# A transformer layer's token sums, load queues, memory norm and weight copies rearranged

## The chip, the cores and the metric

The kernel is one program on one core of a Trainium2 chip. The metric is device microseconds (us) from the start to the end of an execution; lower is better. A core has five engines, each with its own instruction stream: TensorE (PE in the profile; PEld is its weight loads), VectorE (DVE), ScalarE (ACT), GpSimd (POOL) and SyncE (SP). SP computes nothing here: it issues DMAs, which 16 DMA engines carry out. POOL and ACT can issue DMAs as well. An instruction waits on semaphores until its inputs are there, and everything behind it on its engine waits with it.

## The reference, cut to what matters

One layer on a sequence of 1024 tokens and width 1024, in float32: token mixing (a diagonal state-space branch and an eight-head attention with forget gates, each normalised, then one output projection), cross-attention into 256 memory tokens, and a gated feed-forward part.

```python
def rms_norm(x, g):
    return x * lax.rsqrt(jnp.mean(x * x, axis=-1, keepdims=True) + RMS_EPS) * g

mem_n = rms_norm(mem, mem_g)                       # 256 x 1024
proj = rms_norm(x, mix_pre_g) @ w_in               # u | q | k | v | f
y_ssm = s5_mixer(u, ...)                           # ends in a GLU, 512 channels
y_fox = forgetting_attention(q, k, v, f_logit)     # 8 heads x 64 = 512 channels
y_mix = concatenate([rms_norm(y_ssm, ssm_out_g), rms_norm(y_fox, fox_out_g)])
x = x + rms_norm(y_mix @ w_out, mix_post_g)
x = x + rms_norm(memory_cross_attention(rms_norm(x, xa_pre_g), mem_n, wq, wkv, wo), xa_post_g)
x = x + rms_norm(swiglu(rms_norm(x, ffn_pre_g), w_gate, w_up, w_down), ffn_post_g)
```

The two `rms_norm` of the branches need, for each token, the sum of squares over 512 channels. In this kernel the channels lie on partitions, so that sum runs over partitions, and PE makes it: a matmul of 128 tokens' squares with a column of ones.

## The kernel before, in words

Float32 products are made of three matmuls: `split` writes a high part (ACT, L113) and a low part (DVE, L115, or L117 with a gain), and `mm3` (L122 to L124) multiplies high by high, high by low and low by high. So a weight tile goes DMA, ACT, DVE, PE. Tiles have 128 partitions and mostly 512 columns.

A scheduler puts the instructions of each engine in an order from the program's order, priorities and its own costs; `tc.issue_after(x)` keeps what is issued under it behind instruction `x`. The stages, by the times of the profile:

- **0 to 50 us, start-up.** `u_part` multiplies each of eight row blocks of `xT` with a 128x512 block of `w_u`, loaded on SP (`u_load`, L262; `x_fetch`, L205) as PE goes along.
- **50 to 285 us, projections.** `in_proj` makes q, k and v (`qk_tile`, `v_tiles`; q and k go to `qk_d` in DRAM) beside the state-space work. `mem_stats` squares the memory tokens and makes their scale `r_mem`.
- **200 to 500 us, attention.** `fox` goes through 64 units (8 heads `h` x 8 blocks `t` of 128 queries). For a unit, `scores` has PE multiply q and k (L742, L743), DVE add the bias and take the extreme (L749), ACT make the exponentials (L751), and DVE or POOL divide by their sum (L756, L754); then `turn` transposes the unit on PE (L769) and `values` multiplies by v (L780) for each pair of units. `prepare(h + 1)` loads the next head's q and k halves into a buffer with the tag "e", and the bias row `ncb`, on SP (L712, L720, L721). Between units run **fillers**, in this order: the rest of v, `glu` (the GLU of the state-space branch), `mem_load` (loads `memT`, multiplies it by the tokens' scales, L958, and splits it), 16 tiles of `mem_tile` (memory times `wkv`, each result stored to `kv_d` on SP, L972), and rows of `out_ssm` (the state-space half of the output projection, stored to `t1_d` on SP, L854).
- **500 to 593 us, output projection.** For each token block PE multiplies into an x buffer in PSUM; DVE takes it out with the scale `r_f` (L1044), ACT squares it (L1045). Blocks of `build_a(1)` and products with `wo` run between.
- **593 to 785 us, cross-attention** over eight token blocks `j`; `xa_prep(j)` loads the block from `x1_d` (L1069, SP).
- **785 to 1438 us, feed-forward.** `hid` and `wd_sums` prepare combined blocks: `wd_sums` also copies 33 blocks of `w_down` of 256 KB from DRAM to DRAM, to `wd_d` (L1339, SP). These copies depend on nothing, and the scheduler issues them in the start-up.

Squares before: in `glu`, each of eight steps (4 channel blocks `ct` x 2 halves `h`) squares its 128 channels, and `token_sums` makes four matmuls per step (L237), whose result DVE adds to `sv_s` (L239, L241). In `fox`, heads 0 and 1 do the same with two matmuls for each `values`; heads 2 and 3 write squares, and heads 4 to 7 add theirs on POOL (L801) into one tile "d", whose eight sums are taken at the end, before `r_f` can be made.

Of the kernel before, what the change touches and what calls it, by code (L numbers as in the profile page):

```python
# [52 lines left out]
def layer(ctx: ExitStack, tc: tile.TileContext, a, out):  # L53
# [95 lines left out]
    stA, stB, stC = pool, sp, pool  # L149
# [33 lines left out]
    t1_d = dram.tile([L, NC, D], F32, name="t1_d")  # L183
    kv_d = dram.tile([16, P, 256], F32, name="kv_d")
# [48 lines left out]
    def token_sums(sv, sq, first, p0=0, p1=P):  # L233
        n = sv.shape[1]
        ps = g_ps([P, n])
        for j in range(n):
            pe.matmul(ps[:, j:j + 1], sq[:, j * P:(j + 1) * P], ones[p0:p1, 0:1], start=True, stop=True)  # L237
        if first:
            dve.tensor_copy(sv, ps)  # L239
        else:  # L240
            dve.tensor_tensor(out=sv, in0=ps, in1=sv, op=ALU.add)  # L241
# [421 lines left out]
    def glu(ys):  # L663
# [7 lines left out]
        sv = const.tile([P, NT], F32, name="sv_s")  # L671
        sq, sums = tt("d"), []
        for ct in range(4):
            cs = slice(ct * P, (ct + 1) * P)
            hl = slab([P, 2, S])
            for h in range(2):
                hs = slice(h * 512, h * 512 + 512)
# [9 lines left out]
                while sums:  # L687
                    token_sums(*sums.pop())
                act.activation(out=sq[:, hs], in_=y, func=AF.Square)
                sums.append((sv[:, 4 * h:4 * h + 4], sq[:, hs], ct == 0))  # L690
                if h == 1:
                    ys.append(hl)
                yield
        token_sums(*sums.pop())
        ys_stat.append(sv)

    def glu_stats():
        sv, = ys_stat
        tables("natural_log_exp_and_others")
        rsqrt_mean(r_s, sv, 512, 4 * EPS)  # L700


    def fox(yf):
# [3 lines left out]
        def prepare(h):  # L707
# [4 lines left out]
            sp.dma_start(out=ncb, in_=nc_d[h:h + 1, :].broadcast_to([P, S]))  # L712
            heads[h] = (qs, ka, ncb)
            eng = dve if h < 2 else pool
            for hf in range(2):
                hs = slice(hf * 512, hf * 512 + 512)
                qk = tt("d" if h == 0 and hf else "e", [P, 2, 512])
                qd, kd = qk[:, 0], qk[:, 1]
                for rr in (0, 64):
                    sp.dma_start(out=qd[rr:rr + 64], in_=qk_d[h // 2, r0:r0 + 64, hs])  # L720
                    sp.dma_start(out=kd[rr:rr + 64], in_=qk_d[4 + h // 2, r0:r0 + 64, hs])  # L721
                yield
                with behind():
                    act.activation(out=qs[:, hs], in_=qd, func=AF.Copy)
                    eng.tensor_tensor(out=qs[64:128, hs], in0=qd[64:128], in1=qs[64:128, hs].bitcast(F32),
                                      op=ALU.subtract)
                    split(ka[:, 0, hs], ka[:, 1, hs], kd, lo_eng=eng)

        last = []
# [4 lines left out]
        def scores(h, t):  # L734
# [18 lines left out]
            if t in POOL_T and h > 1:  # L753
                pool.tensor_tensor(out=sc[:, :ke], in0=sc[:, :ke], in1=rl.broadcast_to([P, ke]), op=ALU.mult)  # L754
# [17 lines left out]
        def values(h, qc):  # L772
# [17 lines left out]
            if h < HA:  # L790
                act.activation(out=sq, in_=y, func=AF.Square)
                later.append((sv[:, 2 * qc:2 * qc + 2], sq, h == 0, 64 - r0, P - r0))
                return
            if h == HA and qc == 0:
                sums.append(tt("d"))
            total = sums[0][64 - r0:P - r0, qs_]
            if h < HA + 2:
                act.activation(out=total, in_=y, func=AF.Square)
            else:
                act.activation(out=sq, in_=y, func=AF.Square)  # L800
# [35 lines left out]
        while later:  # L836
            token_sums(*later.pop(0))
# [760 lines left out]
```

## Time and profile before

| | |
|---|---|
| Time, median of 3 runs | 1434.43 us (1434.07 to 1434.55) |
| The profiled execution, whole | 1440.18 us |
| Its span (first to last instruction) | 1438.4 us |
| PE busy | 1395.6 us, 97% |
| DVE busy | 1002.3 us, 70% |
| ACT busy | 705.6 us, 49% |
| POOL busy | 398.4 us, 28% |
| Data moved by DMA | 238.42 MB, mean 166 GB/s |

A row such as `60.4 1.36 PE L122 MATMUL g<-whl,slab` has a start, a duration, the engine, the line, the operation and the tiles written and read; a bracket behind it has the idle time just before it and what ended that idle time. A matmul's duration reaches beyond the next one's start, since they are pipelined: what one costs is the distance between starts. `SPq` is a DMA issue on SP. PEclk is the clock that PE was granted, 1.00 being full.

### The profile page before, as it was taken

Reading aid. Unit: us, or ns where it says so; the run is one execution under the profiler, and the core shown is the slowest. Engines: PE = TensorE matmul, PEld = TensorE weight load, DVE = VectorE, ACT = ScalarE, POOL = GpSimd, SP = SyncE. Lnnn points to the kernel's source line nnn. Section 1 sums busy time; section 2 is a strip of 40 time slices with the busy share of each in tenths; the row PEclk is TensorE's granted clock in tenths of the full one; section 3 lists DMA queues with packets and bytes.
Section 4 is the critical chain, followed back from the end, with each engine's and each line's share of the span. In section 5 each row is a group of like instructions: output and inputs, shape, how many; then the busy total and the mean of one; then the engine's idle time right before and its main releaser. Section 6 shows DMA issues by size and latency. Waiting matters only on the chain.

```text
span 1438.4 us, 20783 instructions
## 1 busy us (share of the span) xinstructions
PE 1395.6 (97%) x7422; PEld 1191.4 (83%) x7422; DVE 1002.3 (70%) x1818; ACT 705.6 (49%) x1389; POOL 398.4 (28%) x432
## 2 busy tenths in 40 slices
PE   7999999999999899999999999999999899999997
PEld 6789898889989886788888788888888788888886
DVE  7848957887788877645457677777775766565565
ACT  6363347777888754543434533333333234444441
POOL 0000000022243135001021367667656621000021
PEclk9999999999999999999999999999999999999999
DMA  9625763165644658202327355554455425966544
GB/s 312 216 73 145 201 191 124 39 196 183 194 147 118 172 156 285 91 30 72 105 88 247 134 183 183 183 182 151 166 191 183 146 95 202 339 213 197 176 161 161
DMA packets 112823, 238.42 MB, mean 166 GB/s; under 512 B 11848, under 2 KB 48712, under 8 KB 112592
## 3 DMA queue, kind: packets, MB, share of 16 engines
q1 hardware_dynamic: 96576, 182.01, 39.2%
q0 software_dynamic: 16144, 55.09, 10.8%
q8 instruction: 58, 0.95, 0.3%
q14 instruction: 45, 0.37, 0.1%
HBM read 168.90 MB, written 76.81 MB: 171 GB/s over the span
## 4 chain that ended last, share of the span: by engine, by line
PE 59%; DMA 13%; DVE 11%; POOL 6%; issue 5%; ACT 5%; SPq 1%; DVEq 0%; POOLq 0%; ACTq 0%
PE x L1271 7%; PE x L1526 7%; PE g L1526 7%; PE g L1271 6%; PE g L122 6%; PE g L124 5%; PE g L123 5%; DMA wt<-in_w_down 5%; DMA wt_d<-wt 4%; POOL wt L1345 3%; PE x L123 2%; PE x L124 2%; PE x L122 2%; PE g L769 1%; ACT slab L113 1%
## 5 line engine op out<-in xcount | busy, mean ns | idle before, releaser
L1271 PE MATMUL x<-slab,op 128*128 128x512 f32 x984 | 235.2, 391 | 4.2 <-ACT ev L1287 3.6
L1271 PEld LDWEIGHTS x<-slab,op 128*128 128x128 f32 x984 | 185.7, 189 | 43.8 <-ACT ev L1287 4.1
L1271 PE MATMUL g<-slab,op 128*128 128x512 f32 x744 | 178.7, 389 | 0.0
L115 DVE TENSOR_TENSOR slab<-slab 128x1024 fp32r<-128x1024 f32 (+2 forms) x92 | 110.4, 1208 | 82.3 <-ACT slab L113 80.8
L1271 PEld LDWEIGHTS g<-slab,op 128*128 128x128 f32 x744 | 139.7, 188 | 29.0
L122 PE MATMUL g<-slab,whl 128*128 128x512 f32 (+1 forms) x416 | 151.6, 364 | 0.8 <-DVE slab L115 0.4
L123 PE MATMUL g<-slab,whl 128*128 128x512 f32 (+1 forms) x416 | 148.4, 357 | 0.0
L124 PE MATMUL g<-slab,whl 128*128 128x512 f32 (+1 forms) x416 | 148.0, 357 | 0.0
L113 ACT ACTIVATE slab<-slab 128x1024 fp32r<-128x1024 f32 (+2 forms) x92 | 95.0, 1037 | 104.4 <-DMA slab<-hs_d 81.2
L1526 PE MATMUL g<-slab 128*128 128x512 f32 x462 | 126.6, 389 | 0.0
L1526 PE MATMUL x<-slab 128*128 128x512 f32 x462 | 126.6, 389 | 0.0
L1526 PEld LDWEIGHTS g<-slab 128*128 128x128 f32 x462 | 86.7, 188 | 18.0
L1526 PEld LDWEIGHTS x<-slab 128*128 128x128 f32 x462 | 86.7, 188 | 18.0
L122 PE MATMUL g<-whl,slab 128*128 128x256 f32 (+2 forms) x288 | 86.0, 311 | 11.9 <-ACT whl L113 9.5
L1345 POOL TENSOR_TENSOR wt<-wt 128x256 f32<-128x256 f32 x88 | 73.3, 833 | 73.0 <-DMA wt<-in_w_down 70.6
L113 ACT ACTIVATE op<-ss 128x512 fp32r<-128x512 f32 x60 | 37.6, 629 | 106.3 <-PE g L1271 45.4
L115 DVE TENSOR_TENSOR whl<-raw,whl 128x1024 fp32r<-128x1024 f32 (+2 forms) x61 | 71.9, 1182 | 24.1 <-ACT whl L113 23.7
L122 PEld LDWEIGHTS g<-slab,whl 128*128 128x128 f32 x416 | 78.6, 189 | 12.1 <-ACT whl L113 0.6
L124 PEld LDWEIGHTS g<-slab,whl 128*128 128x128 f32 x416 | 78.4, 189 | 11.6 <-DVE whl L115 0.2
L123 PEld LDWEIGHTS g<-slab,whl 128*128 128x128 f32 x416 | 78.7, 189 | 10.5
L113 ACT ACTIVATE op<-slab 128x512 fp32r<-128x512 f32 x80 | 49.8, 626 | 76.6 <-PE x L1271 40.0
L123 PE MATMUL g<-whl,slab 128*128 128x256 f32 (+2 forms) x288 | 86.7, 301 | 0.0
(394 smaller groups left out, 3192.2 us busy)
## 6 DMA issues: line engine op xcount, KB each, us to landing
hs_d<-ev POOLq DMA_DIRECT2D x77, 256.0 KB, 3.0
slab<-hs_d SPq DMA_DIRECT2D x35, 512.0 KB
wt<-in_w_down SPq DMA_DIRECT2D x44, 256.0 KB
wt_d<-wt POOLq DMA_DIRECT2D x22, 512.0 KB, 3.5
slab<-in_w_gate SPq DMA_DIRECT2D x20, 512.0 KB
slab<-in_w_up SPq DMA_DIRECT2D x20, 512.0 KB
slab<-wt_d SPq DMA_DIRECT2D x20, 512.0 KB
wd_d<-in_w_down SPq DMA_DIRECT2D x33, 256.0 KB
```

Source lines behind the costliest of these rows:

```text
L113: first = act.activation(out=hi, in_=src, func=AF.Copy, scale=1.0 if mul is None else mul)
L115: (lo_eng or dve).tensor_tensor(out=lo, in0=src, in1=hi.bitcast(F32), op=ALU.subtract)
L122: pe.matmul(ps, lh, rh, start=first, stop=False)
L123: pe.matmul(ps, lh, rl, start=False, stop=False)
L124: pe.matmul(ps, ll, rh, start=False, stop=last)
L769: pe.transpose(tp[:, k], sc[:, (k0 + k) * P:(k0 + k + 1) * P], ident)
L1271: pe.matmul(ps, x[:, k], y[:, k], start=first and k + n == 0, stop=k == 3 and n == 2, skip_group_check=not first)
L1345: pool.tensor_tensor(out=o, in0=x, in1=y, op=ALU.subtract)
L1526: pe.matmul(banks[n][j], xo[:, u, js], wo[:, v], start=ends[0] and k == 0, stop=ends[1] and k == 2, skip_group_check=onto is not None)
```

## The change

The program's text changes in these places:

1. **Squares are summed over partitions once.** `glu` goes through its steps half by half; the squares of the four channel blocks are added on DVE in the tile `sq`, and `glu_sums(h)` takes four sums per half. `glu_stats(h)` makes `r_s` half by half, between rows of `out_ssm`. In `fox`, heads 0 and 1 store their squares to `sq_d`, head 2 reads them back as the tile "d", and every later head adds its own on POOL; the sums are taken in the last head, and `r_f` is made in two parts, columns 0 to 5 and 6 to 7.
2. **Queues.** `stB` is ACT, so the 16 stores to `t1_d` (some of the stores of `out_ssm`) and 16 to `kv_d` are issued by ACT. For heads 1 to 7 the loads of q, k and the bias are issued by POOL, as four loads of 64x1024 and the row; from head 3 on they stand behind POOL's multiplication of unit `t` = 1 (`mults`). k lands in the low half of `ka` and is split in place.
3. **Memory norm ahead.** `mem_norm` scales `memT` within `in_proj`, by the tokens' scales on DVE and the gains on ACT, and stores it to `mem_d` on POOL; `mem_load` only loads and splits it.
4. **Copies.** The 33 copies of `w_down` are issued on SP behind the loads of `x1` for blocks 0 to 5.

```diff
-    stA, stB, stC = pool, sp, pool
+    stA, stB, stC = pool, act, pool
...
-    def token_sums(sv, sq, first, p0=0, p1=P):
+    def token_sums(sv, sq):
         n = sv.shape[1]
         ps = g_ps([P, n])
         for j in range(n):
-            pe.matmul(ps[:, j:j + 1], sq[:, j * P:(j + 1) * P], ones[p0:p1, 0:1], start=True, stop=True)
-        if first:
-            dve.tensor_copy(sv, ps)
-        else:
-            dve.tensor_tensor(out=sv, in0=ps, in1=sv, op=ALU.add)
+            pe.matmul(ps[:, j:j + 1], sq[:, j * P:(j + 1) * P], ones[:, 0:1], start=True, stop=True)
+        dve.tensor_copy(sv, ps)
...
-        sv = const.tile([P, NT], F32, name="sv_s")
-        sq, sums = tt("d"), []
-        for ct in range(4):
-            cs = slice(ct * P, (ct + 1) * P)
-            hl = slab([P, 2, S])
-            for h in range(2):
-                hs = slice(h * 512, h * 512 + 512)
+        sq = tt("d")
+        ys_stat.extend((const.tile([P, NT], F32, name="sv_s"), sq))
+        for h in range(2):
+            hs = slice(h * 512, h * 512 + 512)
+            for ct in range(4):
+                cs = slice(ct * P, (ct + 1) * P)
+                if h == 0:
+                    ys.append(slab([P, 2, S]))
+                hl = ys[ct]
...
-                while sums:
-                    token_sums(*sums.pop())
-                act.activation(out=sq[:, hs], in_=y, func=AF.Square)
-                sums.append((sv[:, 4 * h:4 * h + 4], sq[:, hs], ct == 0))
-                if h == 1:
-                    ys.append(hl)
+                act.activation(out=y if ct else sq[:, hs], in_=y, func=AF.Square)
+                if ct:
+                    dve.tensor_tensor(out=sq[:, hs], in0=sq[:, hs], in1=y, op=ALU.add)
+                if (h, ct) == (1, 1):
+                    glu_sums(0)
                 yield
-        token_sums(*sums.pop())
-        ys_stat.append(sv)
-
-    def glu_stats():
-        sv, = ys_stat
-        tables("natural_log_exp_and_others")
-        rsqrt_mean(r_s, sv, 512, 4 * EPS)
+
+    def glu_sums(h):
+        sv, sq = ys_stat
+        token_sums(sv[:, 4 * h:4 * h + 4], sq[:, 512 * h:512 * h + 512])
+
+    def glu_stats(h):
+        hs = slice(4 * h, 4 * h + 4)
+        rsqrt_mean(r_s[:, hs], ys_stat[0][:, hs], 512, 4 * EPS)
...
-            sp.dma_start(out=ncb, in_=nc_d[h:h + 1, :].broadcast_to([P, S]))
...
+            qd, kd = tt("e"), ka[:, 1].bitcast(F32) if h else tt("d")
+            with tc.issue_after(mults[-1].ins) if mults else ExitStack():
+                for rr in (0, 64):
+                    for t_, i in ((qd, 0), (kd, 4)):
+                        (pool if h else sp).dma_start(out=t_[rr:rr + 64], in_=qk_d[i + h // 2, r0:r0 + 64])
+                (pool if h else sp).dma_start(out=ncb, in_=nc_d[h:h + 1, :].broadcast_to([P, S]))
             for hf in range(2):
                 hs = slice(hf * 512, hf * 512 + 512)
-                qk = tt("d" if h == 0 and hf else "e", [P, 2, 512])
-                qd, kd = qk[:, 0], qk[:, 1]
-                for rr in (0, 64):
-                    sp.dma_start(out=qd[rr:rr + 64], in_=qk_d[h // 2, r0:r0 + 64, hs])
-                    sp.dma_start(out=kd[rr:rr + 64], in_=qk_d[4 + h // 2, r0:r0 + 64, hs])
                 yield
                 with behind():
-                    act.activation(out=qs[:, hs], in_=qd, func=AF.Copy)
-                    eng.tensor_tensor(out=qs[64:128, hs], in0=qd[64:128], in1=qs[64:128, hs].bitcast(F32),
+                    act.activation(out=qs[:, hs], in_=qd[:, hs], func=AF.Copy)
+                    eng.tensor_tensor(out=qs[64:128, hs], in0=qd[64:128, hs], in1=qs[64:128, hs].bitcast(F32),
                                       op=ALU.subtract)
-                    split(ka[:, 0, hs], ka[:, 1, hs], kd, lo_eng=eng)
-
-        last = []
+                    split(ka[:, 0, hs], ka[:, 1, hs], kd[:, hs], lo_eng=eng)
+
+        last, mults = [], []
...
-                pool.tensor_tensor(out=sc[:, :ke], in0=sc[:, :ke], in1=rl.broadcast_to([P, ke]), op=ALU.mult)
+                mults.append(pool.tensor_tensor(out=sc[:, :ke], in0=sc[:, :ke], in1=rl.broadcast_to([P, ke]), op=ALU.mult))
...
-            if h < HA:
-                act.activation(out=sq, in_=y, func=AF.Square)
-                later.append((sv[:, 2 * qc:2 * qc + 2], sq, h == 0, 64 - r0, P - r0))
+            act.activation(out=sq, in_=y, func=AF.Square)
+            if h < 2:
+                stC.dma_start(out=sq_d[64 - r0:P - r0, qs_], in_=sq)
                 return
-            if h == HA and qc == 0:
+            if h == 2 and qc == 0:
                 sums.append(tt("d"))
+                stC.dma_start(out=sums[0], in_=sq_d)
             total = sums[0][64 - r0:P - r0, qs_]
-            if h < HA + 2:
-                act.activation(out=total, in_=y, func=AF.Square)
-            else:
-                act.activation(out=sq, in_=y, func=AF.Square)
-                pool.tensor_tensor(out=total, in0=total, in1=sq, op=ALU.add)
+            pool.tensor_tensor(out=total, in0=total, in1=sq, op=ALU.add)
+            if h == NH - 1:
+                later.append((sv[:, 2 * qc:2 * qc + 2], sums[0][:, qs_]))
...
-                    if len(later) > 1 or h >= HA and later:
+                    if len(later) > 1:
                         token_sums(*later.pop(0))
-        while later:
-            token_sums(*later.pop(0))
-        token_sums(sv, sums[0], False)
-        rsqrt_mean(r_f, sv, 512)
+        rsqrt_mean(r_f[:, 0:6], sv[:, 0:6], 512)
+        token_sums(*later.pop(0))
+        rsqrt_mean(r_f[:, 6:8], sv[:, 6:8], 512)
...
+    def mem_norm(r):
+
+        rb = row_bcast(r, 2)
+        for k in range(0, KT, 2):
+            m = t2t([P, 2, 256])
+            sp.dma_start(out=m, in_=a["memT"].rearrange("(k p) m -> p k m", p=P)[:, k:k + 2])
+            dve.tensor_tensor(out=m, in0=m, in1=bc(rb, 1, 2), op=ALU.mult)
+            for i in range(2):
+                act.activation(out=m[:, i], in_=m[:, i], func=AF.Copy, scale=g_mem[:, k + i:k + i + 1])
+            stA.dma_start(out=mem_d[:, k:k + 2], in_=m)
+
...
+            if i == 2:
+                mem_norm(r)
...
-    def mem_load(r, out):
-        rb = row_bcast(r, 2)
-        yield
+    def mem_load(out):
         mh, ml = slab([P, KT, 256]), slab([P, KT, 256])
         for k in range(0, KT, 4):
             m = raw([P, 4, 256])
-            sp.dma_start(out=m, in_=a["memT"].rearrange("(k p) m -> p k m", p=P)[:, k:k + 4])
-            dve.tensor_tensor(out=m, in0=m, in1=bc(rb, 1, 4), op=ALU.mult)
-            for kk in range(4):
-                split(mh[:, k + kk], ml[:, k + kk], m[:, kk], g_mem[:, k + kk:k + kk + 1])
-                if kk % 2:
-                    yield
+            sp.dma_start(out=m, in_=mem_d[:, k:k + 4])
+            split(mh[:, k:k + 4], ml[:, k:k + 4], m)
+            yield
...
-        glu_stats()
-        for _ in mem_load(r_mem[0], mem):
+        tables("natural_log_exp_and_others")
+        glu_stats(0)
+        for h in range(2):
+            for _ in range(2):
+                step(rows)
+                yield
+            if h == 0:
+                glu_sums(1)
+                glu_stats(1)
+        for _ in mem_load(mem):
...
-        sp.dma_start(out=x1, in_=x1_d[j])
+        x1_read.append(sp.dma_start(out=x1, in_=x1_d[j]))
...
-            sp.dma_start(out=wd_d[f, h, p], in_=a["w_down"][2 * p + f][:, h * 512:h * 512 + 512])
+            with tc.issue_after(x1_read[min(k // 4, 5)].ins):
+                sp.dma_start(out=wd_d[f, h, p], in_=a["w_down"][2 * p + f][:, h * 512:h * 512 + 512])
```

What this does to the order of instructions is shown at three places, without the rows' numbers.

SP in the start-up, from the copies on (`wd_d`), `in_w_u` being the blocks for `u_part`, `in_xT` the row blocks of `xT`, `h_d` a small store; before:

```order
L1339 DMA wd_d<-in_w_down 128x512 x6
L205 DMA slab<-in_xT 128x1024
L262 DMA raw<-in_w_u 128x512
L205 DMA slab<-in_xT 128x1024
L1339 DMA wd_d<-in_w_down 128x512 x3
L262 DMA raw<-in_w_u 128x512
L1339 DMA wd_d<-in_w_down 128x512 x14
L262 DMA raw<-in_w_u 128x512
L1339 DMA wd_d<-in_w_down 128x512 x4
L262 DMA raw<-in_w_u 128x512
L1339 DMA wd_d<-in_w_down 128x512 x6
```

And of the change, from the same `h_d` store on (lines are those of the changed text):

```order
L551 DMA h_d<-c 128x112
L207 DMA slab<-in_xT 128x1024
L261 DMA raw<-in_w_u 128x512
L207 DMA slab<-in_xT 128x1024
L261 DMA raw<-in_w_u 128x512 x3
L158 DMA raw<-in_w_f 128x1024
L876 DMA raw<-in_mem 128x1024 x2
```

The 33 copies are gone from between the loads; the last three blocks of `w_u` follow each other, and the weights and memory tokens of the next stage follow them.

SP at the turn to cross-attention, where `x_d` is `x1_d`, `in_post_g` a gain row and `in_wo` the weights of the cross-attention's output; before:

```order
L1069 DMA c<-x_d 128x1024
L948 DMA d<-in_post_g 128x1024
L1069 DMA c<-x_d 128x1024
L158 DMA raw<-in_wo 128x1024 x2
L1069 DMA c<-x_d 128x1024 x5
```

And of the change:

```order
L1084 DMA c<-x_d 128x1024
L1355 DMA wd_d<-in_w_down 128x512
L960 DMA d<-in_post_g 128x1024
L1355 DMA wd_d<-in_w_down 128x512 x2
L158 DMA raw<-in_wo 128x1024
L1084 DMA c<-x_d 128x1024
L1355 DMA wd_d<-in_w_down 128x512 x5
L158 DMA raw<-in_wo 128x1024
L1355 DMA wd_d<-in_w_down 128x512 x4
L1084 DMA c<-x_d 128x1024
```

Three copies now stand ahead of the last but one load of `in_wo`, eight ahead of the last; the rest follow the later blocks' loads.

DVE at the end of attention, from a split of `whl` (weights) on; `sv_f` are the sums, `rst` and `rsv` steps of `r_f`, L1044 takes a block of the output projection out of PSUM; before:

```order
L115 TENSOR_TENSOR whl<-raw,whl 128x1024
L788 TENSOR_TENSOR yt<-g,yt 64x256
L115 TENSOR_TENSOR whl<-raw,whl 128x1024
L117 SCALAR_TENSOR_TENSOR slab<-yt,gains,slab 64x256
L115 TENSOR_TENSOR whl<-raw,whl 128x1024
L241 TENSOR_TENSOR sv_f<-g,sv_f 128x8
L139 TENSOR_SCALAR rsv<-sv_f 128x8
L143 TENSOR_TENSOR rst<-rsy 128x8
L144 TENSOR_TENSOR rst<-rst,rsv 128x8
L117 SCALAR_TENSOR_TENSOR slab<-g,gains,slab 128x256
L145 SCALAR_TENSOR_TENSOR r_f<-rst,rsy 128x8
L1044 SCALAR_TENSOR_TENSOR a<-x,r_f,a 128x512 x2
```

And of the change, where L240 takes the sums out and L1059 is the former L1044:

```order
L240 COPY sv_f<-g 128x2
L139 TENSOR_SCALAR rsv<-sv_f 128x6
L115 TENSOR_TENSOR whl<-raw,whl 128x1024
L143 TENSOR_TENSOR rst<-rsy 128x6
L144 TENSOR_TENSOR rst<-rst,rsv 128x6
L145 SCALAR_TENSOR_TENSOR r_f<-rst,rsy 128x6
L1059 SCALAR_TENSOR_TENSOR a<-x,r_f,a 128x512
L115 TENSOR_TENSOR whl<-raw,whl 128x1024
L1059 SCALAR_TENSOR_TENSOR a<-x,r_f,a 128x512
L789 TENSOR_TENSOR yt<-g,yt 64x256
```

`r_f` for the first six blocks is now made ahead of the last head's last values (`yt`) and of two of the three splits of `whl`; blocks leave PSUM between those splits.

More of the change, by code (lines that the diff above doesn't have):

```diff
@@ L183, in layer @@
     t1_d = dram.tile([L, NC, D], F32, name="t1_d")
+    sq_d = dram.tile([P, S], F32, name="sq_d")
+    mem_d = dram.tile([P, KT, 256], F32, name="mem_d")
     kv_d = dram.tile([16, P, 256], F32, name="kv_d")
@@ L809, in fox @@
         seq = [(h, t) for h in range(NH) for t in range(NT)]
-        HA, sums = 2, []
+        sums = []
         lag = 2
@@ L869, in step @@
                 return
-    ys, yf, gl, ys_stat, r_mem, gate, ssm_made = [], [], [], [], [], [], []
+    ys, yf, gl, ys_stat, gate, ssm_made = [], [], [], [], [], []
     def mem_stats():
@@ L881, in mem_stats @@
         return r
+    def mem_norm(r):
[7 more added lines that the diff above has]
+            stA.dma_start(out=mem_d[:, k:k + 2], in_=m)
     def in_proj():
-        r_mem.append(mem_stats())
+        r = mem_stats()
         yield from k4
@@ L1063, in layer @@
     r3 = const.tile([P, NT], F32, name="r3")
-    xT, xr, pts = {}, {}, {}
+    xT, xr, pts, x1_read = {}, {}, {}, []
     def xa_prep(j):
         x1 = tt("c")
-        sp.dma_start(out=x1, in_=x1_d[j])
+        x1_read.append(sp.dma_start(out=x1, in_=x1_d[j]))
         ss, r = sm(1, "ss"), sm(1, "rxa")
```

## The prediction, made before the changed kernel ran

> **What bounds the kernel now.** I first read the page's busy times, then windows of 40 us, then PE's list of waits.
>
> ```profile
> PE 1395.6 (97%) x7422; PEld 1191.4 (83%) x7422; DVE 1002.3 (70%) x1818; ACT 705.6 (49%) x1389; POOL 398.4 (28%) x432
> ...
> 40.00:80.00 40.00, 37.90 (x174) 31.26 (x173) 32.05 (x79) 17.51 (x38) 0.96 (x1) 0.96 0.54 176
> 240.00:280.00 40.00, 39.20 (x251) 34.18 (x250) 35.17 (x84) 31.49 (x64) 0.05 (x1) 1.00 0.13 41
> 280.00:320.00 40.00, 36.04 (x274) 33.87 (x274) 32.80 (x73) 31.87 (x70) 8.34 (x7) 0.96 0.57 177
> 440.00:480.00 40.00, 39.09 (x309) 36.39 (x307) 34.33 (x80) 35.53 (x82) 14.78 (x15) 1.00 0.39 119
> 480.00:520.00 40.00, 34.18 (x202) 31.10 (x202) 27.51 (x48) 23.54 (x46) 4.28 (x5) 0.87 0.67 180
> 560.00:600.00 40.00, 37.49 (x158) 29.64 (x158) 32.40 (x57) 24.63 (x52) 10.52 (x10) 0.91 0.53 182
> 600.00:640.00 40.00, 40.00 (x191) 33.30 (x190) 16.47 (x48) 15.07 (x43) 0.53 (x1) 1.00 0.07 27
> ...
> PE g L122 <- ACT whl L113: 9.9, 3, 7.4
> PE g L780 <- ACT slab L113: 2.3, 1, 2.3
> PE g L780 <- ACT t L851: 2.1, 2, 1.2
> ```
>
> A window's columns after its length are busy us of PE, PEld, DVE, ACT and POOL, then PE's clock, the DMA engines' share and GB/s. The kernel is bound by PE's work: 97% busy, and from 600 us on nearly without a gap. Time can come from less PE work, or from the few gaps ahead of 600 us; where PE stood, its clock then fell. In attention (240 to 480 us) DVE has 5 to 9 of 40 us free and ACT 4 to 9, so both are near to setting the pace. The sum is made for the profiled execution (1440.2 us, its span 1438.4) and carried over as a difference to the median 1434.4, which is 5.7 us lower.
>
> **A, copies out of the start-up: -4.0.** SP's issues, a piece of the chain of waits, PE's rows, and a window behind them:
>
> ```profile
> 24.89 11.00 SPq L1339 DMA_DIRECT2D wd_d<-in_w_down  x14
> 35.98 0.53 SPq L262 DMA_DIRECT2D raw<-in_w_u  x1
> ...
> 35.98 7.57 DMA raw<-in_w_u
> ...
> 41.83 0.39 PE L124 MATMUL s<-whl,slab 128*128 128x512 f32 x1
> 44.32 1.19 PE L122 MATMUL g<-whl,slab 128*128 128x512 f32 x4 [2.10 <-ACT whl L113]
> ...
> 45.50:48.90 3.40, 3.40 (x10) 2.62 (x9) 3.30 (x16) 0.63 (x1) 0.00 (x0) 0.50 0.97 321
> ```
>
> A block of `w_u` is issued behind 14 copies (11.0 us of SP), lands after 7.57 us on engines 97% busy, and PE stands until then. Matmuls there start 0.23 apart, so 44.32 - 41.83 - 0.23 = 2.3 us are lost; then 3.4 us go at half clock, 1.7 more. Without copies the loads follow each other and land well ahead: -4.0; 0 if the block's buffer or its split is what is late.
>
> The Trainium skill ("TensorE: Matmul & The Clock Gate", "What's actually happening") has the clock fall only after an idle window of some 3.4 us. By it a gap of 2.3 us would cost itself alone, and A would be -2.3; here the window behind a 2.3-us gap shows 0.50, so I keep the row's price.
>
> **B, token sums: -7.** PE rows around two steps of sums:
>
> ```profile
> 273.95 0.95 PE L237 MATMUL g<-ones,d 128*128 128x1 f32 x8
> 274.76 0.49 PE L742 MATMUL s<-slab,a 128*128 128x512 f32 x1
> ...
> 282.00 0.60 PE L237 MATMUL g<-ones,yt 64*128 64x1 f32 x4
> 282.53 0.44 PE L769 MATMUL g<-ident,c 128*128 128x128 f32 x2
> ...
> 274.18 0.68 DVE L684 TENSOR_TENSOR t<-slab 128x512 f32<-128x512 f32 x1
> ```
>
> A step of four matmuls (eight records) takes 0.81 us to the next start, one of two 0.53. Of eight steps in `glu` two remain: 6 x 0.81 = 4.9. The eight steps of heads 0 and 1 go: 8 x 0.53 = 4.2; the eight sums at the end stay. That is 9.1 us of PE. In exchange `glu` gets six additions on DVE, 6 x 0.68 = 4.1 us, nearest to the 240 us window, where 4.8 us of DVE are free: they fit, but barely. I take half of them as given back: -7, between -9 (all hidden) and -5 (none). POOL's eight more additions lie on an engine a third busy.
>
> **C, memory norm ahead: -3.** DVE and PE at that place:
>
> ```profile
> 280.82 3.71 DVE L958 TENSOR_TENSOR raw<-raw,t 128x1024 f32<-128x1024 f32 x2 [0.81 <-ACT t L175]
> ...
> 284.73 0.58 PE L122 MATMUL g<-whl,slab 128*128 128x256 f32 x1 [1.76 <-DVE sv_f L239]
> ...
> 284.40:287.80 3.40, 3.07 (x14) 3.08 (x15) 3.40 (x13) 3.29 (x8) 0.00 (x0) 0.50 0.56 154
> ```
>
> DVE is held for 3.71 us by the two multiplications, a small copy waits behind them, PE waits 1.76 us for the copy, then runs 3.4 us at half clock: 3.5 us. Both the multiplications and that copy leave the place; two splits (bounded by the longer L958 rows, 2 x 1.86) stay. Late next is a block's transposition behind one such split. I take -3, between -3.5 and 0. The norm itself goes to a stage where DVE and ACT have room (32 and 18 of 40 us in 40:80, the nearest row) and PE does not wait for it: 0, at worst +2, a gap with its clock as in C.
>
> **D, `r_f` earlier: -3.** DVE's row where `r_f` is first used, one of its waits ahead, and the end of the stage on PE:
>
> ```profile
> 511.49 1.23 DVE L115 TENSOR_TENSOR whl<-raw,whl 128x1024 fp32r<-128x1024 f32 x1 [2.93 <-ACT whl L113]
> 520.47 1.41 DVE L1044 SCALAR_TENSOR_TENSOR a<-x,r_f,a 128x512 f32<-128x512 f32 x2
> ...
> 572.43 0.50 PE L122 MATMUL x<-whl,b 128*128 128x512 f32 x1 [0.89 <-ACT x L1045]
> 574.13 1.73 PE L122 MATMUL x<-whl,b 128*128 128x512 f32 x4 [0.74 <-ACT whl L113]
> 576.74 0.80 PE L123 MATMUL x<-whl,b 128*128 128x512 f32 x1 [0.88 <-DVE whl L115]
> ...
> 574.60:581.40 6.80, 5.92 (x15) 4.17 (x14) 6.80 (x9) 6.29 (x11) 0.60 (x1) 0.50 0.94 332
> ```
>
> In the new order the first six columns follow the split at 511.49, some 8 us earlier, so DVE takes blocks out while it now stands. Its backlog at the end shows as gaps of 0.89 + 0.74 + 0.88 = 2.5 us and 6.8 us at half clock (3.4): 5.9 us. I take half, since ACT and the weights' splits stand in it too; -6 to +1. The large gap ahead (L780 <- ACT slab, 2.3, and its clock) waits for a weight of `w_out_f` and stays.
>
> **E, stores and table loads on ACT: +2.** The store's issue rows on SP:
>
> ```profile
> L854 SPq DMA_DIRECT2D t_d<-t x16: 360/366/589, 291.2 to 466.3; - x16
> L972 SPq DMA_DIRECT2D kv_d<-t x16: 319/326/332, 306.8 to 378.8; - x16
> ...
> L152 ACT ACT_TABLE_LOAD x5 | 6.4, 1283 | 0.8 <-PEq L1590 0.7
> ```
>
> 16 x 0.366 + 16 x 0.326 = 11.1 us move to ACT, and two more table loads come in beside `glu`, whose Tanh needs the other table: 2.6, together 13.7. If all of it lay on the path it would cost +13.7, if ACT's free time takes it, 0. PE waits for ACT over 200 us of attention in a few rows of about 1 us (L851, 2.1 in two waits), so I stay near the low end: +2. Behind a store on ACT stand the next exponentials and splits; on SP it stood ahead of weight loads.
>
> **F, copies beside `in_wo`: +1.** The issue of the last two such weights, and ACT's split of the last:
>
> ```profile
> 577.97 2.00 SPq L158 DMA_DIRECT2D raw<-in_wo  x2
> ...
> 586.60 1.07 ACT L113 ACTIVATE whl<-raw 128x1024 fp32r<-128x1024 f32 x1
> ```
>
> Eight copies, 2.1 MB, at the 332 GB/s of this place last 6.3 us, and now stand ahead of the last weight, split at 586.6. Its load would land some 1 to 3 us late; with the clock that is up to +4.7, with PE's work ahead 0. The other 25 copies meet 27 GB/s: free.
>
> **G, q and k on POOL: 0.** Rows in the fourth rival. Behind 600 us nothing moves that PE waits for.
>
> **Sum:** -4 - 7 - 3 - 3 + 2 + 1 + 0 = -14: 1426 for the profiled execution, 1420.4 for the median.
>
> **Rivals.**
> 1. *Everything comes* (A, C and D in full, B -9, E and F 0): -4 - 9 - 3.5 - 6 = -22.5, **1412**. For it: ACT and DVE have free time in every window. Against: they wait in rows of single microseconds already.
> 2. *Attention is paced by ACT and DVE*: what PE saves becomes waiting, B is 0, E +7: -4 - 3 - 3 + 7 + 1 = -2, **1432**. For it: 35.5 of 40 us at 440. Against: PE waits there 0.9 us in 40.
> 3. *The copies were not the cause, or collide again*: A is 0, or F +4.7: about -10, **1424**.
> 4. *Loads late on POOL; slower than before.* POOL's issues before, its multiplication of unit 1, and ACT's first use of the loaded q:
>
> ```profile
> L293 POOL DMA_DIRECT2D qk_d<-a x8: 534/537/720, 82.4 to 193.7; - x8
> DMA to landing us min/median/max: 2.9/3.6/10.3
> ...
> 347.74 0.61 POOL L754 TENSOR_TENSOR c<-c,nlr 128x256 f32<-128x256 f32 x1 [13.95 <-DVE nlr L752]
> ...
> 355.67 0.63 ACT L724 ACTIVATE a<-e 128x512 fp32r<-128x512 f32 x1
> ```
>
> The four loads start behind the multiplication, at 348.4, and are needed at 355.7: 7.3 us. At 0.54 an issue and 3.6 to landing they need 5.8: 1.5 us to spare, so G is 0. At the longest landing, 10.3, they are 5 us late. ACT then stands with exponentials behind its copy, five heads over (3 to 7). From 1.2 us late on, with 1.7 of clock, five heads cost 14 and eat the gain; at 2.2 they cost 19: +5, **1439**. Against: the median row, and that ACT now waits 3.1 us here itself.
>
> The Trainium skill ("SBUF — State Buffer", "Who interferes with whom") speaks for this rival: GpSimd cannot write a DMA's descriptors while DVE runs in a mode with both ports. The issues above took 0.54 at a median beside a busy DVE, which does not bear it out; no row has a load on this queue in attention.
>
> **How the numbers follow.** Forecast 0.50; rivals 1 to 4: 0.08, 0.20, 0.12, 0.10. The range goes from 1411, below rival 1, to 1433, above rival 2; it leaves out rival 4 and tails. Faster or slower counts from 0.2% (2.9 us), about what a measurement can tell. Faster: 0.50 + 0.08 + 0.12 and half of rival 2: 0.80. Same: the other half and a little of rival 4: 0.11. Slower: 0.09.
>
> **What would show it.** A: no gap at 42 us, clock 1.00 in 40:80. B: 16 matmuls of sums (32 records). C: no wait for `sv_f`. D: DVE's first `x,r_f` near 511 less the earlier gains, and no half clock at the end of the stage. E: waits of PE for ACT in attention not above 6 us. F: no wait of ACT for `in_wo`. G: no wait of ACT for `qk_d` longer than 1 us. Wrong it is if PE's waits between 240 and 500 us grow by more than 7 us.

## The result and the profile after

| | before | changed |
|---|---|---|
| Time, median of 4 runs each | 1434.49 us | 1453.61 us (1448.42 to 1455.77) |
| Ratio | | 1.0127, 95% interval 1.0097 to 1.0156 |
| Profiled execution, whole | 1440.18 us | 1448.42 us |
| Its span | 1438.4 us | 1446.6 us |

The change is slower by 1.3%, where 1.0% faster was forecast. The two profiled executions lie on the far sides of their medians, so the traces show 8 of the 19 us. The page of the changed kernel, its engines:

```profile
PE 1386.9 (96%) x7342; PEld 1181.2 (82%) x7342; DVE 1016.5 (70%) x1817; ACT 710.3 (49%) x1397; POOL 428.9 (30%) x488
```

PE's busy time fell by 8.7 us, near the 9.1 us worked out for the sums. The work went; waiting came. First windows of the changed kernel, at places of the prediction and at 120 us (columns as there):

```profile
40.00:80.00 40.00, 38.34 (x184) 31.82 (x183) 33.44 (x88) 16.12 (x36) 1.43 (x2) 1.00 0.26 80
120.00:160.00 40.00, 37.29 (x298) 34.31 (x298) 36.30 (x86) 13.75 (x34) 5.93 (x11) 0.96 0.77 211
240.00:280.00 40.00, 35.58 (x204) 29.62 (x203) 37.75 (x88) 33.35 (x67) 5.41 (x10) 1.00 0.28 86
280.00:320.00 40.00, 35.04 (x254) 32.99 (x254) 31.63 (x67) 28.77 (x60) 10.69 (x14) 0.91 0.46 134
560.00:600.00 40.00, 30.56 (x126) 23.10 (x124) 32.73 (x54) 21.12 (x45) 11.03 (x10) 0.91 0.89 287
```

At 40 us the clock is whole. At 120 there is a new loss with its clock, in the GLU (240) PE is busy 35.6 us instead of 39.2, and at 560 PE is idle 9 of 40 us while the DMA engines are 89% busy. From 240 to 500 us PE is busy 242.7 us, against 248.3 before: its sums went, and the stretch holds that much more waiting. PE's waits in the changed kernel:

```profile
PE x L122 <- ACT x L1060: 10.1, 3, 4.7
PE g L122 <- ACT whl L113: 9.0, 3, 7.8
PE s L743 <- DVE nlr L750: 5.7, 6, 1.8
PE x L122 <- ACT whl L113: 2.9, 1, 2.9
PE g L122 <- ACT yt L321: 2.7, 1, 2.7
```

The wait for ACT in the output projection (L1060, the former L1045) went from 2.4 to 10.1 us; scores (L743) now wait for DVE; the waits of 2.9 (weights of `wo`) and 2.7 (`yt` at 133 us) are new.

The stages, each from one PE matmul's start to another's, in the profiled executions (us): *start-up* to the last product of u, *projections* to the first score, *attention* to the last score, then a short stretch, and *output* from the first product of the output projection to the last with `wo`; then cross-attention, here counted to the first feed-forward product into an x buffer (821.7 us before), and the rest:

| kernel | start-up | projections | attention | output | cross-att. | rest |
|---|---|---|---|---|---|---|
| before | 56.7 | 172.2 | 250.2 | 96.8 | 228.8 | 616.7 |
| changed | 53.3 | 179.4 | 249.3 | 107.3 | 228.2 | 611.8 |
| copies only | 53.0 | 174.5 | 248.0 | 101.4 | 229.1 | 611.2 |
| memory norm only | 54.7 | 178.1 | 251.0 | 97.1 | 228.7 | 611.2 |
| sums and queues only | 57.2 | 172.4 | 251.0 | 100.2 | 229.1 | 611.7 |
| changed, copies at start | 56.3 | 176.1 | 249.9 | 100.1 | 229.0 | 615.5 |

The rest, whose text the change leaves as it was but for the place of the copies, lies anywhere from 611 to 617 us in the profiled executions, by a wait near 1140 us that is there in some and not in others; a stage's difference of 1 or 2 us in a single profile is no more than that. The verdicts below go by medians; the table says where. The profiled execution of the norm alone (1439.3 us) is 6.7 us below its median and that of before 5.7 above, so these two spans hardly differ.

### The profile page after: what moved, and what is told of

The parts are those of the page before. It is cut to its first block, busy times and chain, and to the rows that moved or that the text cites. A ratio compares the mean times of both kernels' runs of the same rounds, so it can differ in the third digit from the quotient of the medians.

```text
span 1446.6 us, 20609 instructions
## 1 busy us (share of the span) xinstructions
PE 1386.9 (96%) x7342; PEld 1181.2 (82%) x7342; DVE 1016.5 (70%) x1817; ACT 710.3 (49%) x1397; POOL 428.9 (30%) x488
## 4 chain that ended last, share of the span: by engine, by line
PE 57%; DMA 16%; POOL 8%; DVE 8%; issue 6%; ACT 5%; SPq 0%; POOLq 0%; DVEq 0%; ACTq 0%
PE x L1542 7%; PE g L1542 7%; PE g L122 6%; PE g L124 6%; PE g L123 6%; PE x L1286 5%; DMA wt<-in_w_down 5%; PE g L1286 4%; POOL wt L1361 4%; DMA wt_d<-wt 3%; PE x L122 2%; PE x L123 2%; PE x L124 2%; DMA raw<-in_wkv 1%; POOL ss L1387 1%
## 5 line engine op out<-in xcount | busy, mean ns | idle before, releaser
L113 ACT ACTIVATE slab<-slab 128x1024 fp32r<-128x1024 f32 (+2 forms) x106 | 103.5, 982 | 104.6 <-DMA slab<-hs_d 76.5
L122 PE MATMUL g<-whl,slab 128*128 128x256 f32 (+2 forms) x288 | 89.1, 315 | 12.2 <-ACT whl L113 7.8
L115 DVE TENSOR_TENSOR op<-slab,op 128x512 fp32r<-128x512 f32 x80 | 84.4, 1063 | 17.2 <-ACT op L113 16.6
L124 PE MATMUL g<-whl,slab 128*128 128x256 f32 (+2 forms) x288 | 87.0, 302 | 0.0
```

What stands on the lines that cost most here:

```text
L113: first = act.activation(out=hi, in_=src, func=AF.Copy, scale=1.0 if mul is None else mul)
L115: (lo_eng or dve).tensor_tensor(out=lo, in0=src, in1=hi.bitcast(F32), op=ALU.subtract)
L122: pe.matmul(ps, lh, rh, start=first, stop=False)
L124: pe.matmul(ps, ll, rh, start=False, stop=last)
```

## The experiments

The theory after the first look: four new waits add up (GLU, copies, norm, output projection), and the queues cost nothing. The rivals: one of them is the whole loss, or the queues are. Times are medians; ratios are to the kernel before, on the same chip (1434.2 to 1435.4 us). The change's own interval is 0.3% to each side; with it, a return from the change has to be some 5 to 6 us faster to be told apart from no difference (an estimate from the intervals).

### Parts taken back from the change, one at a time

Copies where the scheduler puts them:

```diff
-            with tc.issue_after(x1_read[min(k // 4, 5)].ins):
-                sp.dma_start(out=wd_d[f, h, p], ...)
+            sp.dma_start(out=wd_d[f, h, p], ...)
```

> The change with the 33 copies of w_down left where the scheduler puts them (start-up), all else as in the change (1453.6 us; before 1434.5). Theory: four new waits add up, and the copies make one of them, beside the last weights of in_wo: the gaps between 588 and 602 us (0.9, 0.8 and 3.1 us, with their half clock, 5 to 7 us in all) go, the start-up's gap with its clock comes back (4 us): -1 to -4, about 1451. Rival (the copies are the whole loss): 1434. Rival (the queues are the whole loss): 1455, by the start-up's gap and nothing else.

1448.1 us, 1.0082 (1.0056 to 1.0107): 5.5 faster than the change by the medians, at the edge of what can be told. In the traces the output stage takes 100.1 instead of 107.3 us, and the start-up's gap came back. The copies are at most a part of the loss, not the whole.

`r_f` made at once:

```diff
-        rsqrt_mean(r_f[:, 0:6], sv[:, 0:6], 512)
         token_sums(*later.pop(0))
-        rsqrt_mean(r_f[:, 6:8], sv[:, 6:8], 512)
+        rsqrt_mean(r_f, sv, 512)
```

> The change with r_f made at once from all eight sums, so that the last sums stand earlier on PE. Theory: the gain row in tile d can be loaded only after the last sums have read that tile; in the change that is at 526.8 us instead of 518.1, and the output projection's multiplications on POOL, its stores and the loads of x behind them are late by 8 us until its end. With the sums earlier the gaps at 560 and 575 us (3.1 and 4.9, with their clock) shrink: -4 to -8, about 1448. Rival (the two parts of r_f brought what I forecast, and something else is late): slower by 2 to 4, about 1456.

1452.4 us, 1.0110 (1.0084 to 1.0137): between the theories, not told apart from no change. PE's row in its trace shows why:

```profile
524.80 0.60 PE L239 MATMUL g<-ones,d 128*128 128x1 f32 x4 [4.62 <-POOL d L799]
```

The last sums stood earlier on PE, but waited 4.6 us for POOL's addition of the last squares.

The memory norm among the fillers again (`mem_norm` out of `in_proj`, `mem_load` as before):

> The change with the memory norm where it was before (multiplied and split among the fillers). Theory: in the change the norm's four tiles take buffers of the projection of v, ACT waits for their stores and PE stands 3.0 us at 130 us, 4.3 with its clock; that goes, the old gap at 283 us (1.8 and clock, 3.5) comes back at most: between -4 and 0, about 1452. Rival (the norm ahead is a gain of 3 us, as forecast): about 1456.5.

1449.5 us, 1.0088 (1.0059 to 1.0118): 4.1 faster by the medians, at the end of what the theory expected and not clear of the noise. In its trace the projections take 174.7 instead of 179.4 us.

The GLU's loop, its eight steps of sums and one `glu_stats` as before:

> The change with the GLU's loop and its eight steps of sums as before; the heads' sums stay as in the change. PE has 4.9 us more work. Theory: the six additions on DVE and the two table loads on ACT made PE wait as long as the sums saved (excess in 240 to 320 us 15.6 instead of 9.4 us): -2 to +1, about 1453. Rival (the sums' saving is there in full): +5, about 1458.5.

1443.5 us, 1.0063 (1.0041 to 1.0085): 10.1 faster, with more work on PE, and clear of the noise. Both expectations missed the size. In its trace attention takes 246.7 instead of 249.3 us.

The stores on SP (`stB = sp`), and apart from that the loads of q, k and bias on SP:

> The change with the 32 stores (t1_d, kv_d) issued by SP as before, all else as in the change (1453.6 us). Theory (the losses are in the GLU, the copies, the norm and the output projection, not in the queues): within 2 us of the change, 1452 to 1455. Rival (the stores hold ACT, 13.7 us as I bounded them): -3 to -8, about 1448.

> The change with the loads of q, k and bias issued by SP for every head, still as four loads of 64x1024 and still behind unit 1's multiplication. Theory: within 2 us of the change, 1452 to 1455, since ACT hardly waits for q in the change. Rival (loads late on the GpSimd queue, my fourth case): -5 or more, 1448 or below.

1453.7 us, 1.0135 (1.0110 to 1.0159), and 1451.6 us, 1.0125 (1.0105 to 1.0145). Neither queue is the loss, as far as these runs can tell (some 5 us).

Norm, GLU and copies taken back together:

> The change with three parts taken back together: the GLU's loop and sums, the memory norm and the place of the copies; what stays is the heads' squares summed once, r_f in two parts, and the queues. Taken one at a time they gave -10, -4 and -5.5 us. Theory, losses that add: 1434, even with before. Rival (each return only shifts the same critical wait, so they don't add): 1440 to 1444.

1439.8 us, 1.0036 (1.0023 to 1.0050): 13.8 faster than the change, where the single returns sum to 19.7. The rival is nearer; but 19.7 is a sum of three uncertain differences, so that the losses overlap is not shown. What is left, the heads' sums, `r_f` and the queues together, still costs 5 us (3 to 7).

### Parts alone

The copies alone on the kernel before; then the same behind later blocks:

```diff
+            with tc.issue_after(x1_read[min(2 + k // 4, 7)].ins):
```

> The kernel before with one part of the change alone: the 33 copies behind the loads of x1 for blocks 0 to 5 (before: 1434.5 us). Theory, from the lengths of the stages in the profiles so far: the start-up to the last product of u gets 3.4 us shorter, the output projection to the last product with wo 6 to 7 us longer (107.3 us in the change, 100.1 with the copies at the start): +3, about 1437.5. Rival (the copies hurt only together with the late sums): -3, about 1431.

> The kernel before with the copies alone, but behind the loads of x1 for blocks 2 to 7, so that none stands ahead of the last weights of in_wo. Theory: the start-up gains its 3.4 us and the stage with in_wo keeps its 96.8: -3.4, about 1431, the best of all. Rival (copies delay the loads of x1 or of the next stage's weights there): 1434 or more.

1437.3 us, 1.0014 (0.9998 to 1.0031), and 1434.2 us, 0.9986 (0.9970 to 1.0001): the first a little slower at most, as its theory has it, the second a little faster at most, nearer to its rival. In the first, the trace shows both parts of the theory. SP, ACT and PE with the copies alone, at the last weights of `wo`:

```profile
579.03 3.07 SPq L1340 DMA_DIRECT2D wd_d<-in_w_down  x4
582.61 0.33 SPq L158 DMA_DIRECT2D raw<-in_wo  x1
...
585.74 1.06 ACT L113 ACTIVATE whl<-raw 128x1024 fp32r<-128x1024 f32 x1 [3.08 <-DMA raw<-in_wo]
...
586.85 1.20 PE L122 MATMUL x<-whl,b 128*128 128x512 f32 x4 [1.42 <-ACT whl L113]
```

The load stands behind copies, ACT waits 3.1 us for it, PE 1.4 us for ACT. And PE ahead of it, in the start-up of the same kernel:

```profile
55.09 0.50 PE L122 MATMUL g<-slab,whl 128*128 128x512 f32 x1 [1.72 <-DVE slab L276]
```

The gap at 44 us is gone, but at 55 us PE waits 1.7 us for the copies of u out of PSUM on DVE, a wait that before did not have. The first score comes at 227.5 us instead of 228.9: of 3.7 us gained by the end of the start-up, 1.4 arrive. With the copies later none do: there the start-up ends 3.2 us earlier, PE has the same wait (1.8 us), and the first score comes at 229.9.

The memory norm alone, and alone but one tile of k earlier (`if i == 1`):

> The kernel before with the memory norm ahead as the only part of the change. Theory: the projections, from the last product of u to the first score, get 5 us longer (179.4 us in the change, 174.7 with the norm taken back, 172.2 before), and the gap at 283 us (1.8 and its clock) goes: +1 to +3, about 1436.5. Rival (forecast): -3, 1431.5.

> The kernel before with the memory norm alone, one tile of k earlier, so that its four t2 tiles are stored before the projection of v needs that tag. Theory (the norm's price is ACT's waits for the stores of tiles that the projection of v needs): the gap of 2.9 us at 130 us and its clock are not there, the projections are back at 172 to 174 us, and the time is near before's or below: 1431 to 1437, against 1446.0 with the norm at its place in the change. Rival (the price is elsewhere: the norm's work on DVE and ACT, or the shorter fillers in attention): 1442 or more.

1446.0 us, 1.0066 (1.0044 to 1.0087), and 1440.0 us, 1.0034 (1.0020 to 1.0048): the first far slower than both expectations, the second between theory and rival. ACT and PE with the norm at the change's place:

```profile
128.57 0.42 ACT L113 ACTIVATE t<-t 128x256 fp32r<-128x256 f32 x1 [2.96 <-DMA mem_d<-t]
131.07 0.47 ACT L298 ACTIVATE t<-g,r_x 128x256 f32<-128x256 f32 x1 [2.08 <-DMA mem_d<-t]
...
133.48 0.59 PE L122 MATMUL g<-whl,slab 128*128 128x264 f32 x1 [2.70 <-ACT yt L323]
```

The norm's tiles and those of the projection of v share a tag (t2); v's tiles wait until the norm's are stored to DRAM, and PE waits for the buffer that ACT can't empty. One tile earlier these three waits are not there, the projections take 174.1 instead of 178.1 us, and 6 us of the 11.5 are back. The other 5.5 were not found. The earlier place differs in a second way, which the run doesn't separate: DVE has more room there (below).

### Within the GLU and the output projection

`r_s` made at once behind the GLU; the additions on POOL instead of DVE; and the first half's `r_s` held behind one table load:

```diff
+        preload = act.preload_act_table_set("natural_log_exp_and_others")
+        tc.keep_in_program_order(preload)
+        with tc.issue_after(preload.ins):
+            glu_stats(0)
```

> The change with both halves' sums taken and r_s made at once behind the GLU, so that ACT loads no table in between; the loop half by half and the six additions on DVE stay. Taking the whole GLU back gave -10 us. Theory (the table loads and ACT's waits around them are the larger share): -5 or more, 1448.5 or below. Rival (DVE's additions are it): -2 to +1, 1452 to 1455.

> The change with the six additions of squares in the GLU on POOL instead of DVE, all else as in the change (1453.6). Theory (DVE is full in the GLU, 37.8 of 40 us, and the 4.1 us of additions is what the loss of 10 us comes from): -4 to -9, about 1447. Rival (the loop half by half and the table loads are the cost): -2 to +2, 1452 to 1456.

> The change with r_s of the first half held behind the last Tanh and one table load, so that ACT loads one table at the GLU's end as before, and not three; sums, loop and additions stay as in the change. Theory (the two table loads inside the GLU, 2.6 us of ACT with what waits behind them, are the loss): -4 to -9, about 1447. Rival (the loop by halves and what it does to the fillers behind it): within 2 us of 1453.6.

1452.4 us, 1.0113 (1.0084 to 1.0143); 1454.8 us, 1.0142 (1.0125 to 1.0159); 1447.4 us, 1.0079 (1.0047 to 1.0111). PE's row in the first:

```profile
291.33 0.98 PE L239 MATMUL g<-ones,d 128*128 128x1 f32 x4 [8.53 <-DVE d L690]
```

It put a wait of its own, 8.5 us for the last addition, in place of what it took, and tells nothing of the loads. The second speaks against the additions on DVE as the cost, though on POOL the last one starts 3 us later (290.4 instead of 287.6 us). By the medians of the third, the table loads are 6 of the 10 us; its five runs lie between 1441.3 and 1451.3, so it can be nearly nothing or all of it. In its trace attention takes 246.2 instead of 249.3 us. ACT in the changed kernel:

```profile
267.84 1.28 ACT L137 ACT_TABLE_LOAD   x1
269.13 0.30 ACT L137 ACTIVATE rsy<-sv_s,epsc 128x4 f32<-128x4 f32 x1
269.34 0.58 ACT L113 ACTIVATE slab<-g 128x512 fp32r<-128x512 f32 x1
269.94 1.28 ACT L138 ACT_TABLE_LOAD   x1
...
273.78 0.67 ACT L684 ACTIVATE t<-g,glub 128x512 f32<-128x512 f32 x1
```

Ahead of the last Tanhs (L684) stand a logarithm and an exponential of 4 columns, each with a load four times its own length or more, and splits of the scores' transpositions behind them.

The GLU's part alone on the kernel before:

> The kernel before with the GLU's new loop, its two steps of sums and r_s by halves as the only part of the change. Theory (the parts add): taken back from the change it gave -10, so alone about +6 to +10, 1441 to 1444. Rival (it costs only where the norm and the copies have already moved the stages): 1432 to 1437, with 4.9 us of PE's work gone.

1434.4 us, 0.9994 (0.9982 to 1.0007): no difference, 4.9 us less work on PE notwithstanding, and with the same two loads among the Tanhs (266.7 and 269.2 us in its trace). From the first Tanh to the last it takes 38.0 us before and 38.3 in the change (43.5 in the trace of the part alone, an execution of 1441.1 us). Of these PE is busy 38.0 before and 33.9 in the change, DVE 35.0 and 36.1, ACT 29.3 and 31.7: the work taken from PE did not become time, and DVE is now nearest to setting the pace. That the part costs nothing alone and 10 us in the change was not expected, and why is not shown.

The last head's values ahead of the weight splits on ACT, in the change and in what was left without norm, GLU and copies; and there `r_f` at once:

```diff
+            wq = [load_w(..., after=ends[-1] if c and (h or d) else None) for d in range(2)]
```

> The change with the splits of the second to fourth weights of wqT on ACT held behind the copy of the last head's last values (as they stand in the order before). Theory: that copy stands in the change behind one more weight split that waits for its load (517.9 instead of 511.5 us), so the last squares, the last sums, the release of tile d, the gain row (527.3 instead of 519.1), POOL's multiplications and the loads of x are all late; with the copy ahead they move 3 to 6 us forward and the gaps at 560 and 575 shrink: -3 to -7, about 1448. Rival (the end of that stage is set by its transfers, which saturate the DMA engines from 540 us on): within 2 us of 1453.6.

> What was left in the run with sums and queues only (1439.8), with the last head's values held ahead of the weight splits on ACT. Theory (the late last sums hold the gain row's tile and with it POOL, the stores and the loads of x): the stage from the first output product to the last product with wo, 100.2 us there and 96.8 before, goes back to 97 to 98: -2 to -4, about 1437. Rival (that stage is set by transfers, or by r_f's two parts): within 1.5 us of 1439.8.

> What was left in the run with sums and queues only (1439.8), with r_f made at once. Theory (the blocks taken out of PSUM between the splits of weights delay those weights, and the stage of the output projection is 3.4 us longer for it): 1435 to 1437, that stage back at 97 to 98 us. Rival (the stores or loads moved to other queues, or the heads' squares): 1439 to 1441.

1451.1 us, 1.0129 (1.0096 to 1.0162); 1440.0 us, 1.0041 (1.0026 to 1.0056); 1440.2 us, 1.0039 (1.0027 to 1.0051). SP's issue of the gain row in the changed kernel, then in the second of these:

```profile
527.25 0.33 SPq L960 DMA_DIRECT2D d<-in_post_g  x1
```

```profile
520.01 0.33 SPq L961 DMA_DIRECT2D d<-in_post_g  x1
```

The row is back near before's time (519.1), and the kernel is no faster; the output stage takes 102.7 us in this trace, 99.1 with `r_f` at once, 100.2 without either. My theory of the late gain row fell, and so did `r_f`'s two parts as the cause. That leaves the rival of the last run, the moved queues or the heads' squares; nothing tells them apart.

## Why the prediction was wrong

By parts alone, the ratios sum to 0.14 + 0.66 - 0.06 + 0.36 = 1.1% (copies, norm, GLU, sums and queues), against 1.27 (0.97 to 1.56) measured. So the parts alone add up to the size, within their intervals. By forecast, the copies (A and F) were -3 and came to +2; the norm (C) -3 and +9.5; sums, `r_f` and queues (B, D, E, G) -8 and some +4. The single steps:

- **C, the norm's new place: the step that failed.** I wrote that it "goes to a stage where DVE and ACT have room", 0, at worst +2. Alone, and net of any gain, the new place costs 9.5 us (0.44 to 0.87%, 6 to 12). I read the room from 40:80, but in the trace the norm's work on DVE and ACT runs from 113 to 126 us, where before has:

```profile
120.00:160.00 40.00, 40.00 (x319) 36.40 (x318) 38.16 (x97) 14.99 (x32) 4.88 (x9) 1.00 0.72 199
```

  DVE is busy 38.2 of 40 us there: it had no room. And its tiles hold buffers of a tag that the next projection was to use; PE stands 2.7 us for that, then goes 3.4 us at half clock, 4.4 us in all. One tile earlier, from 90 to 106 us (DVE busy 6.2 of 20 in 90:110 before), both are better, so their shares stay open, and so does what is left of the price. The gain did not come either. In the change the wait for `sv_f` at 283 us is gone, but in its place stands another for DVE:

```profile
287.21 0.50 PE L743 MATMUL s<-slab,a 128*128 128x512 f32 x1 [1.80 <-DVE nlr L750]
```

  Behind it PE's clock is 0.50 from 288.7 to 295.5 us. With the norm alone, attention did not get shorter (251.0 us, 250.2 before).
- **D, `r_f` earlier: failed in sign.** -3 forecast; the output stage without the copies is 3.3 to 3.4 us longer. `r_f` did come earlier: DVE takes out its first block 17.9 us behind the stage's first product, against 24.4 before, but the stage's end did not follow. PE's waits there for ACT's squares, 2.4 us before, are 6.0 with sums and queues only and 10.1 in the change. POOL's last addition of squares, before and changed:

```profile
515.26 0.80 POOL L801 TENSOR_TENSOR d<-d,yt 64x256 f32<-64x256 f32 x1 [15.06 <-ACT yt L800]
```

```profile
523.00 0.96 POOL L799 TENSOR_TENSOR d<-d,yt 64x256 f32<-64x256 f32 x1 [19.60 <-ACT yt L791]
```

  It is 8 us late, behind ACT, which I had not read from the order there; but putting the values back ahead brought nothing, and neither did `r_f` at once, so the cause of the longer stage stays open.
- **F, copies beside `in_wo`: mis-sized.** +1 forecast; the output stage is 4.6 us longer with the copies alone, 7.2 in the change. I had both ends (4.7) and took a value near the low one. In the change ACT waits for that weight at 601 us:

```profile
601.32 1.06 ACT L113 ACTIVATE whl<-raw 128x1024 fp32r<-128x1024 f32 x1 [1.97 <-DMA raw<-in_wo]
```

- **A, start-up: the mechanism was right, the size not carried through.** The gap and its clock went as forecast (-3.4 in the change), but the next stage waits for DVE instead, and a third of it or nothing reaches the first score. Alone, A and F together made +0.1% (0.0 to +0.3); with the copies later, where F is smaller, -0.1% (-0.3 to 0.0).
- **B, token sums: mis-sized.** PE's work fell by what was worked out; in the GLU none of it is time (0.9994 alone). That DVE and ACT set the pace of attention I had named as rival 2, and took half. What the heads' 4.2 us brought was not run alone.
- **E: right on the stores, wrong on the tables.** The 32 stores cost nothing that could be told (1453.7 us without them on ACT), though I gave 11.1 us as a bound. The two table loads, 2.6 us of ACT, cost about 6 by the medians where the change has them, and the GLU's part alone, with both loads in it, cost nothing.
- **G was right:** POOL's queue carries q and k at no cost that could be told (1451.6 us with them on SP). Rival 4 forecast a slower kernel, but for late loads on POOL, which did not happen.

The clock, which I added as 1.7 us to each gap, is in all of this: its mean over the run is 0.987 in the change's four runs and 0.992 in 29 runs of before (medians). Half a per cent of 1450 us is 7 us, by this estimate more than a third of the loss. But not each gap pays the 1.7 us that I added: in the change three gaps of 2.4 to 3.0 us between 506 and 563 us have a clock of 1.00 behind them.

No version clearly beats before; the copies behind blocks 2 to 7 come nearest (0.9986, up to 1.0001).

## What to carry to other kernels

Where work is moved, read the engines' room at the very place where it will run, not at the nearest convenient row, and look at whose buffers it takes there and what releases them: here the norm's tiles, which go out by a store, held their tag until the store had landed. Where a gap is closed, follow the stage to its end, since the next engine's wait may stand a few microseconds behind it. On this kernel, which PE bounds at 97%, less work for PE was worth nothing in a stage where DVE and ACT are above 80%.

## What the runs showed of the hardware

- A table load took 1.28 us of ACT, and the next instruction started right behind it (267.84 to 269.13 us). Two of them cost 6 us by the medians in the change (1453.6 to 1447.4, barely clear of the noise); the GLU's part alone, which has both and 4.9 us less work on PE, took as long as before (1434.4 against 1434.7).
- A gap of 1.80 us on PE at 285 us was followed by 6.8 us at a granted clock of 0.50 (288.7 to 295.5, changed kernel); gaps of 2.4 us at 506 and 517 us and of 3.0 us at 560 in the same trace were not (1.00 from 490 to 578 us).
- The runs of one kernel spread by 10 to 14 us: before 1430.4 to 1440.6 in 29 runs, memory norm alone 1439.3 to 1453.1 in 10, with mean clocks from 0.987 to 0.993.
- The Trainium skill ("DMA: Bandwidth & Descriptors", "Issuing engines are not separate DMA queues") says that issuing on several engines saves only the issue time. The runs agree: 32 stores and 35 loads between ACT, POOL and SP made at most 2 us by the medians (1451.6 and 1453.7 against 1453.6), which is within the noise of some 5 us.
